# Moving filler matmuls from three carries into the last inverse of a woven recurrence, and loading o from the middle of the last gate

## The chip, the cores and the metric

The kernel runs on one core of a Trainium2 chip. The metric is the device time of one execution in microseconds (us); the time of a kernel is the median of several runs. The profiled execution is one more run, with its own time.

## The reference, cut to what matters

One layer of a diffusion backbone runs over 640 tokens (512 latent tokens of a grid, 128 context tokens) with 1024 features. A projection of the normalised input feeds two branches: an RWKV-7 recurrence in two directions over 8 heads, and a neighbourhood attention over 8 heads. Two gates scale the branches before they are added; a feed-forward network follows.

```python
u_rw, u_na, gate_rw, gate_na = split(h @ w_in)
o_rw, s_new = rwkv_branch(u_rw, ...)          # forward and backward scan, group norm, bonus, gate
o_na = na_latent(...) / na_context(...)
merged = sigmoid(gate_rw) * (o_rw @ w_o_rwkv) + sigmoid(gate_na) * (o_na @ w_o_na)
x = x + g1 * (merged @ w_out)
x = x + g2 * ((silu(h2 @ w1) * (h2 @ w3)) @ w2)
```

All products are held to float32 accuracy: every operand is split into a high and a low part of a reduced type, and a product is three matmuls (high by high, high by low, low by high).

## The kernel before, in words

**Stages.** The first stage normalises the input and makes `h`, held as a high tile `hh` and a low tile `hl` of 128 x 8 x 640 (eight blocks of 128 features, kt 0 to 7). The second does the attention. The third is the recurrence, from about 258 to 676 us of the span, and the change lies there. Then come the output projection and the feed-forward network, to the end.

**The recurrence** works in four passes (`ct` 0 to 3), one per pair of heads. The scan is done in blocks of 64 tokens, in four parts for each pass, written out in program order:

- `main`: products of keys with keys (L1126).
- `inv`, the *inverse*: 30 steps on VectorE that invert the triangular blocks (L1250 and L1254: a multiply and an add for every step), beside them three *jobs* of small matmuls on TensorE (L1145 to L1199, results masked by VectorE in L1157 and L1160), and at its end transposes (L1263, L1265) and two rounds of small matmuls, L1276 and L1290, with copies by ScalarE and VectorE between them.
- `carry`: eight steps that hand the state from block to block. In a step TensorE multiplies (L1324), ScalarE copies (L1327), TensorE multiplies (L1351), ScalarE copies (L1357), TensorE multiplies (L1364), VectorE scales the state (L1376), and the next step begins. Beside it goes `prep`, the preparation of the next pass, on ScalarE and VectorE with some matmuls; `last` finishes it at the last step.
- `out`: the normalised output of the pass (L1396, L1065, L1079, L1410). It is woven into the next pass's inverse; that of the last pass follows the last carry. It stores its chunk to DRAM (`o_d`), for passes 0 to 2; the chunk of the last pass, `o3`, stays in SBUF.

**The filler.** TensorE would stand idle for much of these chains, so a stream of other work (`stream`, `fill`) is woven in. Its units stand in `order`: projections `k`, `r`, `v` of each pass, which must be done before that pass needs them; sixteen gates `g0` to `g15` of 48 matmuls, which read `h`; eight merges `a` of 24 matmuls and eight merges `b` of 18, which read `o`, the outputs of the two branches. A unit has a weight load (`wdma`, from SyncE's queue), a cast to a high and a low part (`wcast`; by `wl` the low part comes from a subtraction on VectorE, `d`, or from an adding DMA on GpSimd's queue, `p`), its matmuls (L197), and an evaluation on ScalarE (gates, L543, stored to `tna_d` or `trw_d` by L544) or VectorE (merges, L1464 and L1467, with the gate loaded back into one of two buffers `mx`, L1450). Casts are issued one unit ahead, loads two units ahead.

**How it is woven.** `weave` walks through the yields of a part; for each it takes one entry of `plan`, whose first number says how many filler matmuls to issue there, and whose others say how far to go on with `out`, `bonus` or `prep`. For a carry the entries go in threes, one for each yield of a step. TensorE, VectorE, ScalarE and GpSimd execute in this program order; the order of SyncE's queue is chosen by the framework's scheduler. When the passes are done, `need` issues what is left of the stream without anything between.

**Where `o` lies.** `o` is a pair of tiles, high and low, in the same memory as `hh` and `hl`: `hilo` gives the same two buffers of 8 blocks. Blocks 0 to 3 are the attention's output, 4 to 6 the first three passes' output. `o_load(0, 6)` is issued when the last gate's matmuls are done (the unit before `a0`), and its DMAs wait until TensorE has read `hh` and `hl` for the last time; `o_load(6, 7)` follows when the third pass's output is stored.

**After the stream,** `last_gen` multiplies the last chunk (L1576, on `o3`) and evaluates it with VectorE (L1577, L1579), woven with the output projection.

Of the kernel before, what the change touches and what calls it, by code (L numbers as in the profile page):

```python
# [7 lines left out]
F32 = mybir.dt.float32  # L8
F32R = mybir.dt.float32r
AF = mybir.ActivationFunctionType  # L10
# [4 lines left out]
P = 128  # L15
NT = 640
NS = 512
H2 = 320
# [6 lines left out]
TCARGS = dict(schedule_with_timeline_sim=True)  # L25

PRM = dict(
    order=("l0 l1 k0 r0 v0 l2 g0 g1 g2 k1 g3 r1 g4 g5 v1 g6 g7 k2 r2 g8 g9 v2 g10 g11 k3 r3 g12 g13 v3 g15 g14 a0 a1 a2 a3 a4 a5 a6 a7 "
     "b0 b1 b2 b4 b3 b5 b6 b7"),
    plan=(  # L30
        "22.0 0.0 2.0 4.0",
        ("0.0.0 2.0.0 2.0.1 10.0.0 2.0.0 2.0.1 2.0.1 2.0.1 2.0.1 2.0.1 10.0.0 2.0.0 2.0.0 10.0.0 2.0.0 2.0.0 "
         "2.0.0 10.0.0 2.0.0 2.0.0 2.0.0 2.0.0 2.0.0 2.0.0 2.0.0 2.0.0 2.0.0 2.0.0 2.0.0 2.0.0 5.0.0 24.0.0 "
         "20.0.0 10.0.0 8.0.0 8.0.0 0.0.0"),
        ("10.0 1.0 12.1 0.2 0.0 8.1 6.2 0.0 8.1 6.2 0.0 8.1 12.2 0.0 8.1 6.2 0.0 8.1 6.2 0.0 7.1 5.2 0.0 9.1 "
         "6.2 6.0"),
        "22.0 2.0 2.0 2.0",
        ("0.0.0 0.0.0 2.0.1 10.0.0 1.0.0 2.1.1 2.1.1 2.1.1 2.1.1 1.1.1 10.0.0 3.0.0 2.0.0 2.0.0 2.1.0 2.1.0 "
         "2.0.0 10.0.0 2.0.0 2.1.0 2.1.0 2.1.0 2.1.0 2.1.0 12.1.0 2.1.0 2.1.0 2.1.0 2.0.0 2.1.0 5.0.0 24.0.0 "
         "20.0.0 10.0.0 8.0.0 8.0.0 0.0.0"),  # L40
        ("10.0 0.0 8.1 6.2 0.0 8.1 6.2 0.0 8.1 6.2 0.0 8.1 6.2 0.0 8.1 6.2 0.0 7.1 6.2 0.0 8.1 6.2 0.0 8.1 "
         "6.2 6.0"),
        "22.0 2.0 0.0 5.0",
        ("0.0.0 10.0.0 2.0.1 10.0.0 2.0.0 2.1.1 2.1.1 2.1.2 2.1.1 2.1.0 10.0.0 2.0.0 2.0.0 2.0.0 2.1.0 2.1.0 "
         "2.0.0 10.0.0 2.0.0 2.1.0 2.1.0 3.1.0 4.1.0 2.1.0 2.1.0 2.1.0 2.1.0 4.1.0 2.1.0 2.0.0 5.0.0 24.0.0 "
         "18.0.0 8.0.0 9.0.0 8.0.0 0.0.0"),
        ("10.0 0.0 8.1 14.2 0.0 8.1 6.2 0.0 8.1 6.2 0.0 0.1 6.2 0.0 8.1 6.2 0.0 8.1 6.2 0.0 8.1 6.2 0.0 8.1 "
         "6.2 6.0"),
        "22.2 0.0 4.0 6.0",
        ("0.0.0 16.1.0 8.1.1 9.0.0 2.1.0 8.1.1 8.1.1 8.1.1 8.1.1 0.1.1 0.1.0 0.0.0 0.1.0 0.1.0 0.1.0 0.1.0 "  # L50
         "6.1.0 7.1.0 6.1.0 6.0.0 6.0.0 6.0.0 0.0.0 6.0.0 6.0.0 7.0.0 6.0.0 6.0.0 6.0.0 6.0.0 6.0.0 6.0.0 "
         "11.0.0 8.0.0 8.0.0 2.0.0 0.0.0"),
        ("10.0 0.0 8.1 6.2 0.0 8.1 4.2 0.0 8.1 6.2 0.0 8.1 6.2 0.0 8.1 6.2 0.0 8.1 6.2 0.0 8.1 6.2 0.0 8.1 "
         "14.2 6.0"),
        "2 0 6 6 6 4 4 5 2 0 5 1 1 0 0"),
    qp=((0, 0, 7, 6, 7), (2, 5, 4, 4, 3, 2, 5, 3, 1)), ada=2, pa=1, pd=0,
    lw=(0, 0, 0, 0, 0, 2, 2, 2, 2, 2, 2, 2, 2, 2, 2, 2),
# [50 lines left out]
def body(ctx: ExitStack, tc: tile.TileContext, xs, xp, cols, consts, w_ada, b_row, w_rw, w_qkv,  # L108
# [3 lines left out]
    pe, act, dve, pool, sp = nc.tensor, nc.scalar, nc.vector, nc.gpsimd, nc.sync  # L112
# [12 lines left out]
    hp = right_pool(hstack, "hp")  # L125
# [9 lines left out]
    def nm(s):  # L135
        cn[0] += 1
        return f"{s}_{cn[0]}"
# [72 lines left out]
    halves = ((0, H2), (H2, NT))  # L210
# [11 lines left out]
    tna_d = dp.tile([8, P, NT], F32, name="tna_d")  # L222
# [89 lines left out]
    weights(ctx, WST, 2)  # L312
    o, mt = [], []

    def hilo(n):
# [219 lines left out]
    def gate_gen(i, w, ps_, gsb, gtag):  # L535
        dst = trw_d[i] if i < 8 else tna_d[i - 8]
        for (a, b) in ((0, H2), (H2, NT)):
            t = gsb.tile([P, H2 if gtag == "fl" else 643], F32, tag=gtag, bufs=2, name=nm(gtag))[:, :H2]
            ps = ps_()
            yield from feat_gen(ps, w, (hh, hl), 8, a, b)  # L540

            def rest(t=t, ps=ps, a=a, b=b):
                act.activation(t, ps[:, :H2], AF.Tanh, scale=0.5)  # L543
                sp.dma_start(dst[:, a:b], t)  # L544

            later(rest)

    def c64(ap, d=0):
# [171 lines left out]
    def unit(g, e):  # L720

        i, eng = int(g[1:]), eng_of(e)
        if g[0] in "ab":
            return 24 if g[0] == "a" else 18, lambda: merge_load(g[0], i), \
                lambda wt: merge_cast(*wt, eng), lambda w: merge_gen(g[0], i, w)
        if g[0] == "g":
            return 48, lambda: wdma(w_rw[15 + i]), lambda w: wcast(w, eng), \
                lambda w: gate_gen(i, w, flps, sb, gtag[-1])
# [305 lines left out]
    with ExitStack() as s3:  # L1034
# [395 lines left out]
        def o_load(a, b):  # L1430

            if not o:
                o.extend(hilo("o"))
            for q in range(a, b):
                for t, t_d in zip(o, o_d):
                    sp.dma_start(t.bitcast(F32)[:, q, :], t_d[q])

        def mt_tile(c8):
            if c8 < 4:
# [268 lines left out]
    u = {}  # L1708
# [290 lines left out]
```

## Time and profile before

| | us |
|---|---|
| median of 3 runs | 1192.29 |
| lowest, highest | 1192.16, 1193.37 |
| profiled execution | 1191.72 |
| its span | 1189.7 |
| TensorE busy in it | 1124.1 |
| VectorE busy | 777.5 |
| ScalarE busy | 530.5 |
| mean granted TensorE clock | 0.985 |

A row of the page's groups, of the order in time or of the waits names the line of the kernel, the engine (PE is TensorE, PEld its weight loads, DVE VectorE, ACT ScalarE, POOL GpSimd, SP SyncE), the operation, and output <- inputs; in the order in time the first two numbers are start and length, in us from the span's start, and brackets hold the idle time of the engine before the row and what ended it. Rows that follow each other are merged, `xN` counts them. A row of a window gives its length, the busy time of PE, PEld, DVE, ACT and POOL (with instruction counts), the granted TensorE clock, the share of time that the DMA engines were busy, and GB/s.

### The profile page before, as it was taken

Reading aid. Unit: us, or ns where it says so; the run is one execution under the profiler, and the core shown is the slowest. Engines: PE = TensorE matmul, PEld = TensorE weight load, DVE = VectorE, ACT = ScalarE, POOL = GpSimd, SP = SyncE. Lnnn points to the kernel's source line nnn. Section 1 sums busy time; section 2 is a strip of 40 time slices with the busy share of each in tenths; the row PEclk is TensorE's granted clock in tenths of the full one; section 3 lists DMA queues with packets and bytes.
Section 4 is the critical chain, followed back from the end, with each engine's and each line's share of the span. In section 5 each row is a group of like instructions: output and inputs, shape, how many; then the busy total and the mean of one; then the engine's idle time right before and its main releaser. Section 6 shows DMA issues by size and latency. Waiting matters only on the chain.

```text
span 1189.7 us, 26921 instructions
## 1 busy us (share of the span) xinstructions
PE 1124.1 (94%) x11160; PEld 998.3 (84%) x11160; DVE 777.5 (65%) x1630; ACT 530.5 (45%) x1053; POOL 205.1 (17%) x273
## 2 busy tenths in 40 slices
PE   6999999999999999999599799989999999999998
PEld 4688877789888988888488678889899989998997
DVE  4564455559469658836474675888568757775675
ACT  4444666554564664565133342654224422442340
POOL 1162244320111211111101250100001000000000
PEclk9999999999999999999799999999999999999999
DMA  9762767553333514433654851312312231232122
GB/s 335 265 117 84 244 216 230 191 146 98 103 93 84 153 50 104 123 93 79 200 138 110 245 218 54 107 49 79 104 57 86 89 107 54 89 100 90 59 75 103
DMA packets 61906, 149.42 MB, mean 126 GB/s; under 512 B 7732, under 2 KB 23732, under 8 KB 61784
## 3 DMA queue, kind: packets, MB, share of 16 engines
q1 hardware_dynamic: 55592, 131.56, 33.6%
q0 software_dynamic: 5328, 14.94, 6.8%
q8 instruction: 88, 1.44, 0.5%
q10 hardware_dynamic: 864, 1.20, 0.3%
q14 instruction: 34, 0.28, 0.1%
HBM read 118.41 MB, written 14.32 MB: 112 GB/s over the span
## 4 chain that ended last, share of the span: by engine, by line
PE 65%; DVE 8%; ACT 3%; DMA 2%; issue 1%; SPq 0%; ACTq 0%; DVEq 0%; POOLq 0%
PE f L1718 23%; PE acc L284 17%; PE fl L197 13%; DMA wlo<-wst 1%; DVE pr L1250 1%; PE w L1324 1%; PE w L1351 1%; DVE RL L1254 1%; PE mm L197 1%; PE w L1364 1%; PE w L1336 1%; PE w L1148 1%; DMA o<-o_d 1%; PE w L1196 1%; PE w L1126 1%
## 5 line engine op out<-in xcount | busy, mean ns | idle before, releaser
L1718 PE MATMUL f<-t,whi 128*128 128x320 f32 x640 | 141.4, 309 | 0.0
L1718 PE MATMUL f<-b,whi 128*128 128x320 f32 x608 | 136.5, 312 | 3.6 <-ACT b L185 1.8
L284 PE MATMUL acc<-whi,u 128*128 128x512 f32 (+1 forms) x448 | 136.0, 385 | 0.0
L197 PE MATMUL fl<-h,whi 128*128 128x320 f32 x704 | 126.5, 319 | 0.8 <-issue 0.8
L197 PEld LDWEIGHTS fl<-h,whi 128*128 128x128 f32 x704 | 106.1, 188 | 5.6 <-issue 0.9
L173 ACT CAST whi<-wst 128x1024 fp32r<-128x1024 f32 (+2 forms) x86 | 81.5, 953 | 64.7 <-PE acc L284 32.5
L1718 PEld LDWEIGHTS f<-t,whi 128*128 128x128 f32 x640 | 107.1, 188 | 0.0
L1718 PEld LDWEIGHTS f<-b,whi 128*128 128x128 f32 x608 | 103.0, 190 | 4.8 <-ACT b L185 2.2
L1718 PE MATMUL f<-t,wlo 128*128 128x320 f32 x320 | 98.9, 309 | 0.0
L284 PEld LDWEIGHTS acc<-whi,u 128*128 128x128 f32 x448 | 83.5, 188 | 16.7
L1718 PE MATMUL f<-b,wlo 128*128 128x320 f32 x304 | 94.7, 312 | 1.4 <-DVE wlo L1762 1.4
L1759 ACT CAST whi<-ws 128x1024 fp32r<-128x1024 f32 x40 | 42.0, 1051 | 108.7 <-PE f L1718 48.5
L1773 POOL TENSOR_TENSOR ws<-wst 128x512 f32<-128x512 f32 x20 | 28.2, 1409 | 341.3 <-DVE wlo L1762 226.7
L175 DVE TENSOR_TENSOR wlo<-wst,whi 128x1024 fp32r<-128x1024 f32 (+1 forms) x49 | 62.0, 1274 | 37.2 <-ACT whi L173 36.6
L284 PE MATMUL acc<-wlo,u 128*128 128x512 f32 (+1 forms) x224 | 86.3, 385 | 0.0
L284 PE MATMUL acc<-whi,h 128*128 128x512 f32 x240 | 78.0, 399 | 1.2 <-DVE h L398 1.1
L172 POOL DMA_DIRECT2D wlo<-wst x37 | 32.6, 881 | 232.4 <-ACT wlo L171 212.9
L1558 DVE SCALAR_TENSOR_TENSOR tt<-acc,G 128x512 f32<-128x512 f32 (+1 forms) x51 | 34.7, 681 | 50.5 <-PE acc L284 50.5
L197 PE MATMUL fl<-h,wlo 128*128 128x320 f32 x352 | 66.5, 321 | 0.0
L197 PE MATMUL fl<-o,whi 128*128 128x320 f32 x224 | 46.3, 337 | 16.8 <-DMA o<-o_d 10.0
L1759 ACT CAST whi<-wst 128x1024 fp32r<-128x1024 f32 (+1 forms) x48 | 41.3, 869 | 42.3 <-PE acc L284 37.6
L1718 PEld LDWEIGHTS f<-t,wlo 128*128 128x128 f32 x320 | 60.1, 188 | 0.0
(333 smaller groups left out, 2539.1 us busy)
## 6 DMA issues: line engine op xcount, KB each, us to landing
wst<-in_w_dram SPq DMA_DIRECT2D x66, 512.0 KB
wst<-in_w_rw_dram SPq DMA_DIRECT2D x31, 512.0 KB
wa<-in_w_ada_dram SPq DMA_DIRECT2D x24, 512.0 KB
wlo<-wst POOLq DMA_DIRECT2D x22, 512.0 KB, 4.5
f<-in_w_ada_dram SPq DMA_DIRECT2D x16, 512.0 KB
wst<-in_w_qkv_dram SPq DMA_DIRECT2D x12, 512.0 KB
o<-o_d SPq DMA_DIRECT2D x14, 320.0 KB
x<-in_xs_dram SPq DMA_DIRECT2D x8, 512.0 KB
```

The lines of the kernel that those rows point to most:

```text
L172: pool.dma_start(lo[:, :n].bitcast(F32), st[:, :n], accum_op=ALU.add)
L173: act.copy(hi[:, :n], st[:, :n])
L175: dve.tensor_tensor(out=lo[:, :n], in0=st[:, :n], in1=hi[:, :n].bitcast(F32), op=ALU.subtract)
L197: pe.matmul(ps[:, :t1 - t0], w[:, a:a + 128], x[:, k0 + kt, t0:t1], start=n == 0, stop=n == 3 * nk - 1)
L284: pe.matmul(pss[i][:, a:b], lhs(x, kt, ts_), w[:, cs_], start=ki == 0 and n == 0, stop=ki == last and n == 2)
L1126: pe.matmul(t[r0:r0 + 32, 64 * i:64 * i + 64], S.BK[l // 10][own, l % 10, 0, 32 * bk:32 * bk + 32], V(AG[own, l, h, :], [[0, 2], [1, 32]], ...
L1148: pe.matmul(pr[h][hrows[h ^ i], o_], x[hrows[h], :], R_[hrows[h], l, :], start=True, stop=True)
L1196: pe.matmul(pt[h][hrows[h ^ i], o_], S.BK[l // 10][hrows[h], l % 10, i, :], idh(h), start=True, stop=True)
L1558: dve.scalar_tensor_tensor(out=tt, in0=ps[:, a:b], scalar=c, in1=G[:, g, sl], op0=ALU.mult, op1=ALU.mult)
L1718: pe.matmul(ps[:, :H2], w_[:, c_], x_[:, kt, :], start=first and kt + n == 0, stop=last and kt == 3 and n == 2, skip_group_check=more)
L1759: act.copy(r[0][:, :width], src())
L1773: eng_x(PRM["se"][i - 1]).tensor_tensor(out=o_, in0=x, in1=y, op=op)
```

## The change

Four edits go together.

The plan's entries for the first three carries are two fillers lower at nearly every place (108 matmuls in all); the entries of the last pass's `main` and inverse are written anew: four at nearly every step of the inverse, 44 behind the last step. `order` brings `v1`, `k2`, `v2`, `k3`, `v3` forward among the gates, so that each projection still comes in time.

`hilo` no longer gives one tile of eight blocks but two of four (`hp_t`), behind a small class `Two` that indexes them as one.

The last gate, `g14` (`lg=14`), is issued by `gate2_gen`: it goes by blocks, both halves of the tokens for kt 0 and 1, then for 2 and 3, and so on, with three matmuls for every block, instead of one half of the tokens after the other. After its first 24 matmuls it calls `o_load(0, 4)`; `o_load(4, 6)` is called at its end.

`wl` has the low parts of the weights of all eight `b` merges made by VectorE instead of the adding DMA, and that of `a4` the other way round.

```diff
-     order=("l0 l1 k0 r0 v0 l2 g0 g1 g2 k1 g3 r1 g4 g5 v1 g6 g7 k2 r2 g8 g9 v2 g10 g11 k3 r3 g12 g13 v3 g15 g14 a0 ...
+     order=("l0 l1 k0 r0 v0 l2 g0 g1 g2 k1 g3 r1 g4 v1 g5 g6 k2 r2 g7 v2 g8 g9 k3 r3 g10 v3 g11 g12 g13 g15 g14 a0 ...
...
-        ("10.0 1.0 12.1 0.2 0.0 8.1 6.2 0.0 8.1 6.2 0.0 8.1 12.2 0.0 8.1 6.2 0.0 8.1 6.2 0.0 7.1 5.2 0.0 9.1 "
-         "6.2 6.0"),
+        ("6.0 1.0 8.1 0.2 0.0 6.1 4.2 0.0 6.1 4.2 0.0 6.1 10.2 0.0 6.1 4.2 0.0 6.1 4.2 0.0 5.1 5.2 0.0 "
+         "7.1 4.2 4.0"),
...
-        "22.2 0.0 4.0 6.0",
-        ("0.0.0 16.1.0 8.1.1 9.0.0 2.1.0 8.1.1 8.1.1 8.1.1 8.1.1 0.1.1 0.1.0 0.0.0 0.1.0 0.1.0 0.1.0 0.1.0 "
-         "6.1.0 7.1.0 6.1.0 6.0.0 6.0.0 6.0.0 0.0.0 6.0.0 6.0.0 7.0.0 6.0.0 6.0.0 6.0.0 6.0.0 6.0.0 6.0.0 "
-         "11.0.0 8.0.0 8.0.0 2.0.0 0.0.0"),
+        "22.3 0.1 4.1 6.2",
+        ("0.0.0 4.1.0 4.1.1 4.1.1 4.1.1 4.1.1 4.1.1 4.1.1 4.1.1 4.1.0 4.1.0 4.1.0 4.0.0 4.0.0 4.0.0 "
+         "4.0.0 4.0.0 4.0.0 4.0.0 4.0.0 4.0.0 4.0.0 4.0.0 4.0.0 4.0.0 4.0.0 4.0.0 4.0.0 4.0.0 4.0.0 "
+         "4.0.0 44.0.0 0.0.0 6.0.0 6.0.0 12.0.0 0.0.0"),
...
-    wl="dddddddddppppppppppppppppppppppppppdpppppppppppp", nu=9, jo=(2, 0, 1), na=(
+    wl="dddddddddppppppppppppppppppppppppppppppdddddddd", nu=9, lg=14, jo=(2, 0, 1), na=(
...
+    def hp_t(n, i, j):
+        return hp.tile([P, 4, NT], F32R, tag=f"hp{i}{j}", bufs=1, name=f"{n}{i}{j}")
...
     def hilo(n):
-        return [hp.tile([P, 8, NT], F32R, tag=f"hp{i}", bufs=1, name=f"{n}{i}") for i in range(2)]
+        return [Two([hp_t(n, i, j) for j in range(2)]) for i in range(2)]
...
+    def gate2_gen(i, w, ps_, gsb, gtag):
+        dst = trw_d[i] if i < 8 else tna_d[i - 8]
+        ps = [ps_(), None]
+        for kts in ((0, 1), (2, 3), (4, 5), (6, 7)):
+            for hf, (a, b) in enumerate(halves):
+                if ps[hf] is None:
+                    ps[hf] = ps_()
+                for kt in kts:
+                    for n, (u, x) in enumerate(((w[0], hh), (w[0], hl), (w[1], hh))):
+                        pe.matmul(ps[hf][:, :H2], u[:, kt * 128:kt * 128 + 128], x[:, kt, a:b],
+                                  start=kt == 0 and n == 0, stop=kt == 7 and n == 2)
+                        yield
+            if kts[1] == 3:
+                o_load(0, 4)
...
                     if i + 1 < len(order) and order[i + 1] == "a0":
-                        o_load(0, 6)
+                        o_load(4, 6)
...
         def o_load(a, b):
             if not o:
-                o.extend(hilo("o"))
+                o.extend(Two([]) for _ in range(2))
             for q in range(a, b):
-                for t, t_d in zip(o, o_d):
-                    sp.dma_start(t.bitcast(F32)[:, q, :], t_d[q])
+                for i, (t, t_d) in enumerate(zip(o, o_d)):
+                    if len(t.ts) == q // 4:
+                        t.ts.append(hp_t("o", i, q // 4))
+                    sp.dma_start(t[:, q, :].bitcast(F32), t_d[q])
```

The other two carries' entries change in the same way as the one shown.

More of the change, by code (lines that the diff above doesn't have):

```diff
@@ L27 @@
 PRM = dict(
[L28 to L29 removed]
+    order=("l0 l1 k0 r0 v0 l2 g0 g1 g2 k1 g3 r1 g4 v1 g5 g6 k2 r2 g7 v2 g8 g9 k3 r3 g10 v3 g11 g12 g13 g15 g14 a0 a1 a2 "
+     "a3 a4 a5 a6 a7 b0 b1 b2 b4 b3 b5 b6 b7"),
     plan=(
         "22.0 0.0 2.0 4.0",
[L32 to L54 removed]
@@ new lines @@
+        ("8.0 0.0 6.1 4.2 0.0 6.1 4.2 0.0 6.1 4.2 0.0 6.1 4.2 0.0 6.1 4.2 0.0 5.1 4.2 0.0 6.1 4.2 0.0 "
+         "6.1 4.2 4.0"),
+        "22.0 2.0 0.0 5.0",
+        ("0.0.0 10.0.0 2.0.1 10.0.0 2.0.0 2.1.1 2.1.1 2.1.2 2.1.1 2.1.0 10.0.0 2.0.0 2.0.0 2.0.0 2.1.0 "
+         "2.1.0 2.0.0 10.0.0 2.0.0 2.1.0 2.1.0 3.1.0 4.1.0 2.1.0 2.1.0 2.1.0 2.1.0 4.1.0 2.1.0 2.0.0 "
+         "5.0.0 24.0.0 18.0.0 8.0.0 9.0.0 8.0.0 0.0.0"),
+        ("6.0 0.0 6.1 12.2 0.0 6.1 4.2 0.0 6.1 4.2 0.0 0.1 4.2 0.0 6.1 4.2 0.0 6.1 4.2 0.0 6.1 4.2 0.0 "
+         "6.1 4.2 4.0"),
@@ L313, in body, with __init__, __getitem__ @@
     o, mt = [], []
+    def hp_t(n, i, j):
+        return hp.tile([P, 4, NT], F32R, tag=f"hp{i}{j}", bufs=1, name=f"{n}{i}{j}")
+    class Two:
+        def __init__(self, ts):
+            self.ts = ts
+        def __getitem__(self, x):
+            return self.ts[x[1] // 4][x[0], x[1] % 4, x[2]]
     def hilo(n):
-        return [hp.tile([P, 8, NT], F32R, tag=f"hp{i}", bufs=1, name=f"{n}{i}") for i in range(2)]
+        return [Two([hp_t(n, i, j) for j in range(2)]) for i in range(2)]
     hh, hl = hilo("h")
@@ L546, in gate_gen, with rest @@
             later(rest)
+    def gate2_gen(i, w, ps_, gsb, gtag):
[12 more added lines that the diff above has]
+                o_load(0, 4)
+        def rest(hf, a, b):
+            t = gsb.tile([P, H2 if gtag == "fl" else 643], F32, tag=gtag, bufs=2, name=nm(gtag))[:, :H2]
+            act.activation(t, ps[hf][:, :H2], AF.Tanh, scale=0.5)
+            sp.dma_start(dst[:, a:b], t)
+        for hf, (a, b) in enumerate(halves):
+            later(lambda hf=hf, a=a, b=b: rest(hf, a, b))
     def c64(ap, d=0):
```

10 lines of the change are left out of this document (9 added, 1 removed).

## The prediction

> **What bounds the kernel now.** I read the page first, then PE's waits, then PE's order in time through the recurrence, and last the sums of a few stretches. Every time below is us.
>
> The page: busy shares, and the span in 40 slices of 29.7.
>
> ```profile
> PE 1124.1 (94%) x11160; PEld 998.3 (84%) x11160; DVE 777.5 (65%) x1630; ACT 530.5 (45%) x1053; POOL 205.1 (17%) x273
> PE   6999999999999999999599799989999999999998
> PEclk9999999999999999999799999999999999999999
> ```
>
> TensorE is the bound almost everywhere. After the start, the slices that are not full are those from 565 to 595, 654 to 684 and their neighbours: the last inverse, and the end of the recurrence. In the first of them the clock was low too. PE's waits name what was late (line, releaser, total, times, longest):
>
> ```profile
> PE fl L197 <- DMA o<-o_d: 10.0, 1, 10.0
> PE fl L197 <- DVE mt L1464: 4.7, 1, 4.7
> PE fl L1576 <- ACT o L185: 3.1, 1, 3.1
> PE w L1324 <- DVE ZV L1376: 1.5, 1, 1.5
> PE w L1351 <- ACT x L1327: 1.4, 4, 0.4
> PE w L1364 <- ACT ZV L1357: 0.4, 1, 0.4
> ```
>
> The first two lie in the last inverse, the third at the recurrence's end; the last three are all that the carries wait. Four stretches summed (length, busy PE, weight loads, DVE, ACT, POOL, then the granted clock): the third pass's inverse, the fourth's, a busy carry step, and the stretch from the fourth carry's end to the first matmul on the last chunk of `o`.
>
> ```profile
> 449.38:500.51 51.13, 47.87 (x1013) 44.10 (x1012) 44.28 (x151) 27.93 (x54) 8.61 (x18) 1.00 0.38 103
> 550.22:621.94 71.72, 54.91 (x1032) 50.38 (x1031) 46.46 (x158) 22.84 (x47) 11.22 (x15) 0.88 0.53 155
> 427.72:432.65 4.93, 4.49 (x63) 3.77 (x62) 1.13 (x3) 4.30 (x12) 1.03 (x2) 1.00 0.63 140
> 661.48:679.03 17.55, 12.67 (x81) 11.30 (x80) 9.98 (x20) 6.62 (x14) 5.29 (x4) 1.00 0.86 251
> ```
>
> The fourth inverse does what the third does, with 24 filler matmuls more (208 against 184, counted in the order of issue), and takes 20.6 longer: it waits, and part of it runs at half clock. That is the loss that the change can reach.
>
> **The unit of the sum.** What moves is filler: 128x128 by 320 matmuls. Twelve of them back to back, from the first row's start to the second's:
>
> ```profile
> 599.16 1.33 PE L197 MATMUL fl<-o,whi 128*128 128x320 f32 x8
> 600.92 1.33 PE L197 MATMUL fl<-o,whi 128*128 128x320 f32 x8
> ```
>
> 1.76 for 12 is 0.147 each. The order of issue of both kernels gives the counts. The first three inverses and carries lose 5+32, 2+34 and 4+44 fillers, 121 in all (108 is what the plan takes out; the rest is a knock-on of the stream's own order). The last inverse keeps 208, but 175 of them are gates (54 before) and 33 merges (154 before). The last carry keeps 126. What follows it has 177 merges instead of 56. No matmul is added or dropped, so the change moves 121 x 0.147 = 17.8 of PE work from the first three carries to the end of the recurrence, and the time changes only by waits.
>
> **First three carries: -17.8 + 5.** A carry step is a ring: L1324 on PE, a copy on ACT, L1351, two copies on ACT (L1357), L1364, two multiplies on DVE (L1376), the next L1324. Filler covers the second and third hand-over: 8 and 6 before, 6 and 4 after. In a quiet step of the fourth carry:
>
> ```profile
> 636.94 0.45 PE L1324 MATMUL w<-ZV,AG 128*64 128x64 f32 x8
> 638.31 0.55 ACT L1357 COPY ZV<-w 64x128 f32<-64x128 f32 x2 [0.55 <-PE w L1351]
> 639.55 0.45 PE L1364 MATMUL w<-ZV,TG 128*64 128x64 f32 x8
> 640.05 0.61 DVE L1376 TENSOR_TENSOR ZV<-w,Dt 64x128 f32<-64x128 f32 x2 [2.81 <-PE w L1364]
> 641.25 0.45 PE L1324 MATMUL w<-ZV,AG 128*64 128x64 f32 x8
> ```
>
> ACT is done at 638.86 and PE takes the result at 639.55: 0.69 in hand. DVE is done at 640.66, PE goes on at 641.25: 0.59. Two fillers less take 0.29 from each, so a quiet step shortens from 4.31 to 3.7 without a wait. The first three carries are not quiet: the next pass's preparation queues on ACT and DVE. In the busy step above ACT works 4.30 of 4.93 and PE already waits 0.44 of it; with four fillers less PE needs 3.9, and the step will not go below ACT's 4. Nearly all steps elsewhere have room, so I charge 0.2 on each of 24 steps, 5 in all. The bounds: nothing (the quiet step), and all 17.8 (a rival below).
>
> **Last inverse: -14.7.** Gates read `h`, which is there; merges read `o`, which must come from DRAM into the place of `h`. Before, the load could start only as the last gate ended:
>
> ```profile
> 562.20 8.15 SPq L1436 DMA_DIRECT2D o<-o_d  x12
> 573.93 3.07 PE L197 MATMUL fl<-o,whi 128*128 128x320 f32 x7 [10.04 <-DMA o<-o_d]
> 574.72 0.50 PEld L197 LDWEIGHTS fl<-o,whi 128*128 128x128 f32 x2 [0.29 <-DMA o<-o_d]
> 576.36 0.29 PEld L197 LDWEIGHTS fl<-o,whi 128*128 128x128 f32 x1 [0.30 <-DMA o<-o_d]
> ```
>
> The six loads of the low halves went out ahead of the first high half, so PE had its first pair only at 573.9; from then a load landed every 0.81 (574.72 to 576.36 are two). Everything in PE's order behind the first merge waited with it, the output step of the third pass (L1079) and so DVE with its inverse among it. After, gates fill this inverse nearly to its end. The two new tiles of four blocks are free after 24 matmuls of the last gate, and eight loads go out in pairs. Between that point and the first merge PE has 24 gate matmuls (3.5) and the small ones of L1276 (1.5, first row below), so 5.0. The first load lands no sooner than a small transfer does (second row, the last number), and no later than the rows above allow:
>
> ```profile
> 612.20 1.47 PE L1276 MATMUL w<-f,Nt 32*32 32x32 f32 x80
> wlo<-wst POOLq DMA_DIRECT2D x8, 192.0 KB, 3.9
> ```
>
> 3.9 from issue to landing, or 11.7 for seven loads less six at 0.81, 6.8. The eighth is then there 9.6 to 12.5 after the release. Without waits PE would want it at about 6, so it waits 3.6 to 6.5; I take 4, near the lower end because these loads find the queue empty. ACT would hold PE nearly as long at this place: the next matmuls (L1290) need four copies of L1276's results, and among them ACT's order has two gate outputs and the next merge's two casts: eight operations of about the size of this one, some 4 together:
>
> ```profile
> 638.88 0.53 ACT L171 ACTIVATE wlo<-wst 128x384 fp32r<-128x384 f32 x1
> ```
>
> The two waits run side by side and are counted once.
>
> The inverse then costs the third one's PE work, 47.9, 24 fillers more (3.5), the wait (4), and 1.6 for what follows a wait, below: 57.0 against 71.7. DVE does not forbid that: 44.28 busy in the third inverse, which holds projections of the next pass that the fourth has not. Bounds: 53 (hardly a wait) and 61 (6.5, half clock and some of the third inverse's own 3.3 of waits).
>
> SP's queue holds the fourteen loads in one run, ahead of the last gate's stores and the weights of the third merge. The first two merges, 48 fillers woven into the inverse's end and the carry's start, cover those weights, and POOL adds their low parts as before. I cost this at nothing; without that cover PE would wait for one such addition, up to 3.9 less what is left of the merges.
>
> **What a wait costs beside itself.** Two stretches of one window each, with busy PE and clock:
>
> ```profile
> 341.80:345.20 3.40, 1.87 (x25) 1.43 (x23) 2.56 (x6) 3.33 (x6) 0.86 (x1) 1.00 0.02 5
> 345.20:348.60 3.40, 3.40 (x30) 3.03 (x30) 2.38 (x4) 2.23 (x6) 0.00 (x0) 0.51 0.78 154
> 614.90:618.30 3.40, 2.06 (x39) 1.86 (x43) 3.35 (x8) 0.51 (x2) 0.00 (x0) 1.00 0.39 100
> ```
>
> A wait of 1.53 was followed by 3.4 at half clock; 1.34 idle left the clock whole. So 3.4 at half clock, 1.7 of work lost, follows a wait of about 1.5 in such a window; 0.2 a step does not bring it, the wait for `o` may, hence the 1.6. The Trainium skill, "TensorE: Matmul & The Clock Gate", section "What's actually happening", has the array fall to half rate only after at least one idle window of about 3.4. The trace differs, since 1.53 idle was enough here; by the Trainium skill's rule the sum would be 1.6 lower, and I go by the rows.
>
> **End of the recurrence: +17.8 - 3.3 + 2 = +16.5.** The 121 merges come as one block with nothing woven in. Before, PE waited for the last chunk of `o` at the end, and DVE was behind with weights:
>
> ```profile
> 675.34 0.60 PE L197 MATMUL fl<-o,wlo 128*128 128x320 f32 x3
> 680.41 1.21 DVE L175 TENSOR_TENSOR wlo<-wst,whi 128x1024 fp32r<-128x1024 f32 x1
> 681.55 1.27 DVE L1577 SCALAR_TENSOR_TENSOR pre<-pre,fl 128x320 f32<-128x320 f32 x3
> ```
>
> From the last merge's end (675.94) to DVE's first step of the next stage (681.55) passed 5.6. After, the chunk is long ready when the block ends; DVE has one weight split (1.21) and two steps of 0.49 left, 2.3 with the first matmuls. That returns 3.3. The block itself is 7.7 units of 18 matmuls (2.65). A unit's DVE work is four steps and a split, which moves from a POOL addition to DVE:
>
> ```profile
> 663.05 0.49 DVE L1464 SCALAR_TENSOR_TENSOR mx<-mx,fl 128x320 f32<-128x320 f32 x1 [1.38 <-PE fl L197]
> 663.57 0.49 DVE L1467 TENSOR_TENSOR mt<-mt,mx 128x320 f32<-128x320 f32 x1
> 601.94 0.68 DVE L175 TENSOR_TENSOR wlo<-wst,whi 128x512 fp32r<-128x512 f32 x1
> ```
>
> 4 x 0.49 + at most 0.68 is 2.6, as long as PE's: level, so 0.25 a unit, 2 in all (0 to 10, second rival).
>
> **Sum.** -17.8 + 5 - 14.7 + 16.5 = -11.0. The profiled execution took 1191.7, its span 1189.7; the median of the runs is 1192.3. -11.0 gives 1181.3 on the median. The inverse's bounds give 4 to either side, half of the carries' lower bound and of an equal step above 2.5, the block 1 (its 10 is a rival): 1174 to 1189 for the forecast alone.
>
> **Rivals.**
> 1. The split load buys little: `o` still lands 10 late, as in the old row. Then the inverse is 47.9 + 3.5 + 10 + 1.7, 63.1, and the time 1187.4. For it: the same 2.6 MB at the same rate. Against: five of the ten are covered by PE work behind the release, and the pairs are ordered.
> 2. The closing block is paced by transfers. Two `mx` buffers make a ring over two units: load, then DVE's 2.6. At 3.9 a load it is 3.3 a unit, at 5, 3.8; with 5 the block loses 1.15 x 7.7 = 8.9 instead of 2: 1188.2. For it: the stretch from 661 had DMA at 0.86. Against: the loads for the next stage come before the block now.
> 3. The carries keep their length, and it gets slower. If ACT's queue paces the steps, removed filler becomes waiting, all 17.8 of it: 12.8 more than forecast, 1194.1, and the two later carries, which end without a wait today, each bring a window at half clock as the first does: 1197.5. It decides where the steps lose over 0.66 each on average. For it: the busy step. Against: the quiet one has 0.59 and 0.69 in hand, and over a whole carry ACT has room:
>
> ```profile
> 405.00:448.00 43.00, 42.32 (x572) 37.29 (x569) 21.26 (x38) 28.20 (x72) 7.39 (x11) 1.00 0.32 81
> ```
>
> 28.2 of 43, which 36 fillers less (5.3) leave at 28.2 of 38 at the most.
>
> **Chances.** Forecast 0.68, rivals 0.10, 0.10 and 0.12. From no change a measurement here can tell about 0.2%, 2.4. Faster: the forecast and the first two rivals without their tails, 0.86; slower: most of the third, 0.10; the same, 0.04. The range for 8 in 10 takes the forecast's own, the first two rivals, and 2 below it for terms that fall together: 1172 to 1190.
>
> **What would show it.** Right: the wait for `o` at 3 to 6 in pieces, late in an inverse of about 57; carry steps of 3.7 to 4.4 with small waits on L1327, L1357, L1376; a block of 138 merges of about 22 behind the last output step; no wait on the last chunk. Wrong: half clock inside the first three carries, an `o` wait near 10, or PE waiting for DVE or `mx` through the block.

## The result, and the profile after

| | before | after |
|---|---|---|
| median of 4 runs, us | 1192.43 | 1200.47 |
| lowest, highest | 1192.16, 1193.37 | 1199.02, 1202.57 |
| profiled execution, its span | 1191.72, 1189.7 | 1199.02, 1197.2 |

The changed kernel is slower: ratio 1.0066, 95% interval 1.0051 to 1.0081, some 8 us. The forecast was 1181.3 in 1172 to 1190.

The page of the changed kernel, its busy times and the same two rows of slices (29.9 us each):

```profile
PE 1130.5 (94%) x11160; PEld 1003.5 (84%) x11160; DVE 778.9 (65%) x1637; ACT 527.9 (44%) x1046; POOL 196.3 (16%) x266
PE   6999999999998998899989989999999999999998
PEclk9999999999999998899989999999999999999999
```

The hole in the last inverse (565 to 595 before) has closed, and so has the one at the recurrence's end but for a digit. But where the page before has nines, eights have come: from 359 to 389 and, in the clock too, from 449 to 509. Those lie in the second and the third inverse. (The eights from 599 to 629 belong to the end of the last inverse; the one from 688 to 718 lies in the last chunk and what follows it.) (The passes are counted from one here: the inverses of passes one to four are the first, second, third and last inverse.)

The recurrence in stretches (length, busy PE, weight loads, DVE, ACT, POOL, clock, DMA share, GB/s). Of before, the first carry, second inverse, second carry and third carry, which the prediction did not show:

```profile
305.23:354.86 49.63, 47.49 (x625) 41.93 (x624) 23.63 (x44) 29.75 (x75) 6.14 (x10) 0.97 0.33 86
354.86:403.09 48.23, 46.56 (x1009) 43.22 (x1008) 43.94 (x150) 27.02 (x53) 10.13 (x21) 1.00 0.42 109
403.09:449.38 46.29, 45.53 (x619) 40.11 (x618) 24.21 (x43) 28.57 (x73) 7.83 (x12) 1.00 0.35 90
500.51:550.22 49.71, 48.57 (x636) 42.77 (x635) 23.61 (x44) 29.54 (x76) 7.16 (x12) 1.00 0.36 93
```

Of after, from the first carry to the last inverse without a gap, and then the stretch from the last carry's end to the first matmul on the last chunk of `o`:

```profile
304.94:351.54 46.60, 43.22 (x592) 37.50 (x591) 23.47 (x45) 28.03 (x72) 6.78 (x12) 0.96 0.25 66
351.54:405.06 53.52, 48.49 (x1006) 44.77 (x1005) 46.58 (x153) 26.57 (x53) 7.48 (x17) 0.97 0.38 102
405.06:448.02 42.96, 40.64 (x585) 35.07 (x584) 21.26 (x39) 27.63 (x71) 8.18 (x12) 1.00 0.25 68
448.02:509.75 61.73, 51.94 (x1008) 48.09 (x1008) 47.34 (x154) 26.29 (x52) 8.82 (x20) 0.89 0.37 95
509.75:554.63 44.88, 43.17 (x602) 37.46 (x602) 23.61 (x43) 29.87 (x76) 5.99 (x11) 1.00 0.32 80
554.63:613.12 58.49, 53.24 (x1022) 48.18 (x1021) 40.63 (x144) 22.54 (x44) 8.21 (x13) 0.91 0.56 170
651.68:686.06 34.38, 31.80 (x202) 30.59 (x201) 23.51 (x49) 9.41 (x18) 3.94 (x3) 0.95 0.66 202
```

Set against each other, in us:

| stretch | before | after | change | forecast |
|---|---|---|---|---|
| three carries | 145.6 | 134.4 | -11.2 | -12.8, inverses' 11 fillers included |
| second and third inverse | 99.4 | 115.3 | **+15.9** | in the line above |
| last inverse | 71.7 | 58.5 | -13.2 | -14.7 |
| last carry's end to the last chunk | 17.6 | 34.4 | +16.8 | +16.5, with what follows it |
| all the rest | | | -0.8 | 0 |

The rest is the span's difference, 7.5, less the lines above. Three lines came near the forecast. The miss stands in two inverses that the sum took as unchanged but for a few fillers. By the rows above, 9.9 of their 15.9 is TensorE idle (14.8 for 4.9) and 6.0 is longer busy time: some 17 of the two inverses ran at half clock (clock 0.97 and 0.89), and none of them before. TensorE's waits (line, releaser, total, times, longest) name what is late in them:

```profile
PE w L1182 <- DVE out L1446: 8.3, 3, 3.6
PE fl L197 <- issue: 4.5, 2, 3.5
PE fl L1612 <- DVE tr L1613: 3.3, 1, 3.3
PE w L1385 <- ACT x L1361: 3.2, 5, 1.0
PE fl L197 <- DMA o<-o_d: 2.2, 5, 0.6
PE w L1358 <- DVE ZV L1410: 2.1, 2, 1.8
PE fl L197 <- DMA wlo<-wst: 1.8, 1, 1.8
```

Lines of the kernel's part on the recurrence are 34 higher than before: L1182 is L1148, the third job's matmuls; L1446 is L1412, the last multiply of the output step; L1160 is L1126, the tiny matmuls of `main`. The wait between these two was 2.0 in all before, a row that the list of waits in the prediction leaves out:

```profile
PE w L1148 <- DVE out L1412: 2.0, 1, 2.0
```

The 10.0 on `o` has become 2.2. The 4.5 on "issue", a wait for nothing that the profile shows, has a piece of 3.5.

**The first of the two.** VectorE in the third inverse (start, length):

```profile
485.00 0.34 DVE L533 SCALAR_TENSOR_TENSOR kt__622<-U,C,kt__622 128x128 f32<-128x128 f32 x1
...
485.71 0.74 DVE L533 SCALAR_TENSOR_TENSOR kt__622<-U,C,kt__622 128x512 f32<-128x512 f32 x1
486.49 0.75 DVE L535 SCALAR_TENSOR_TENSOR kt__622<-U,C,kt__622 128x512 f32<-128x512 f32 x1
487.16 0.48 DVE L1446 TENSOR_TENSOR out<-w,out 128x320 f32<-128x320 f32 x1
...
490.21 0.48 DVE L1446 TENSOR_TENSOR out<-w,out 128x320 f32<-128x320 f32 x1
```

and TensorE there:

```profile
487.70 0.33 PE L1182 MATMUL w<-R__2889,f 64*64 64x64 f32 x2 [2.02 <-DVE out L1446]
490.74 0.38 PE L1182 MATMUL w<-R__2889,f 64*64 64x64 f32 x3 [2.71 <-DVE out L1446]
```

L533 and L535 are the four steps that shift the projection `k3` by a token, 2.2 together. They stand ahead of both L1446; L1446 empties a PSUM buffer `w`; the third job's matmuls wait for one. (In the second inverse the steps of `k2`, at 383.3 to 385.5, stand ahead of the second L1446 alone, and its wait of 3.6 follows.) Before, the same steps came behind both L1412, here in the third inverse:

```profile
482.37 0.48 DVE L1412 TENSOR_TENSOR out<-w,out 128x320 f32<-128x320 f32 x1
...
486.88 0.35 DVE L522 SCALAR_TENSOR_TENSOR kt__620<-U,C,kt__620 128x128 f32<-128x128 f32 x1 [0.31 <-ACT kt__620 L521]
```

In fillers: `k2` ended at the 85th of its inverse before and at the 74th after, `k3` at the 102nd and at the 79th. `order` moved `k2` one gate of 48 fillers forward and `k3` two, while the passes ahead of them had lost only 37 and 73 fillers.

**The second.** The order in time of all engines, three rows:

```profile
447.33 0.88 POOL L172 DMA_DIRECT2D wlo<-wst  x1 [1.73 <-ACT wlo L171]
...
451.48 0.46 PE L1160 MATMUL w<-AG,f 64*32 64x64 f32 x32
...
455.45 1.49 PE L197 MATMUL fl<-h,wlo 128*128 128x320 f32 x5 [3.51 <-issue]
```

The matmul at 455.45 needs nothing new. What the trace does have is TensorE's program being loaded: DMA queue q8 moves 88 blocks of 16 KiB in the execution, one for every 256 of TensorE's 22,517 records (weight loads, matmuls and some 200 semaphore instructions). The queues (packets, MB, share) from 443.5 to 452.9, with the adding DMA's time to landing, and from there to 454.1:

```profile
q0 software_dynamic: 144, 0.52, 35.4%
q1 hardware_dynamic: 280, 0.48, 13.6%
q14 instruction: 1, 0.01, 0.5%
...
wlo<-wst POOLq DMA_DIRECT2D x1, 512.0 KB, 5.6
```

```profile
q1 hardware_dynamic: 19, 0.05, 29.4%
q8 instruction: 1, 0.02, 5.0%
```

No block for TensorE arrives in the first stretch. The adding DMA (q0) landed at 452.9; the block was loaded from 453.02 to 453.97, and 1.48 later TensorE went on. It had stopped behind record 10177, 193 past a multiple of 256.

### The profile page after: what moved, and what is told of

The parts are those of the page before. It is cut to its first block, busy times and chain, and to the rows that moved or that the text cites. A ratio compares the mean times of both kernels' runs of the same rounds, so it can differ in the third digit from the quotient of the medians.

```text
span 1197.2 us, 26923 instructions
## 1 busy us (share of the span) xinstructions
PE 1130.5 (94%) x11160; PEld 1003.5 (84%) x11160; DVE 778.9 (65%) x1637; ACT 527.9 (44%) x1046; POOL 196.3 (16%) x266
## 4 chain that ended last, share of the span: by engine, by line
PE 51%; DVE 4%; DMA 2%; ACT 2%; issue 2%; SPq 1%; POOL 0%; DVEq 0%; ACTq 0%; POOLq 0%
PE f L1754 21%; PE acc L284 16%; PE fl L197 8%; DMA wlo<-wst 1%; DMA tr<-trw_d 1%; DMA o<-o_d 1%; PE w L1182 1%; DVE hq L1713 0%; PE w L1398 0%; PE w L1358 0%; DVE t L186 0%; PE w L1385 0%; PE w L1370 0%; PE w L1230 0%; PE w L1415 0%
## 5 line engine op out<-in xcount | busy, mean ns | idle before, releaser
L197 PE MATMUL fl<-h,whi 128*128 128x320 f32 x672 | 122.1, 323 | 1.0 <-issue 1.0
L197 PEld LDWEIGHTS fl<-h,whi 128*128 128x128 f32 x672 | 103.2, 191 | 5.4 <-issue 1.2
L175 DVE TENSOR_TENSOR wlo<-wst,whi 128x1024 fp32r<-128x1024 f32 (+1 forms) x56 | 65.1, 1169 | 36.6 <-ACT whi L173 36.1
L1594 DVE SCALAR_TENSOR_TENSOR tt<-acc,G 128x512 f32<-128x512 f32 (+1 forms) x51 | 34.7, 680 | 51.1 <-PE acc L284 51.1
L172 POOL DMA_DIRECT2D wlo<-wst x30 | 26.5, 882 | 238.8 <-ACT wlo L171 234.8
L1754 PEld LDWEIGHTS f<-b,wlo 128*128 128x128 f32 x304 | 57.4, 189 | 2.5 <-DVE wlo L1798 2.5
```

Of the source, the lines that this page charges most:

```text
L172: pool.dma_start(lo[:, :n].bitcast(F32), st[:, :n], accum_op=ALU.add)
L175: dve.tensor_tensor(out=lo[:, :n], in0=st[:, :n], in1=hi[:, :n].bitcast(F32), op=ALU.subtract)
L197: pe.matmul(ps[:, :t1 - t0], w[:, a:a + 128], x[:, k0 + kt, t0:t1], start=n == 0, stop=n == 3 * nk - 1)
L1594: dve.scalar_tensor_tensor(out=tt, in0=ps[:, a:b], scalar=c, in1=G[:, g, sl], op0=ALU.mult, op1=ALU.mult)
L1754: pe.matmul(ps[:, :H2], w_[:, c_], x_[:, kt, :], start=first and kt + n == 0, stop=last and kt == 3 and n == 2, skip_group_check=more)
```

## The experiments

All ratios are to the kernel before on the same chip, with 95% intervals. The two inverses are given as second / third, against 48.2 / 51.1 before and 53.5 / 61.7 after. They are read from one profiled execution each, and half clock moves them: the third inverse of e7 and e8, whose program there is the changed kernel's, took 59.3 and 59.5, with 6.8 at half clock instead of 13.7. A difference of 2 in a third inverse says little. The runs e1 to e3 and e5 to e10 start from the changed kernel. Where two runs are set against each other, it is by their medians; the kernel before had medians of 1192.3 to 1193.4 beside them, so 1 of such a difference can be the chip's.

**e1: later shifts.**

```diff
+        lag = 24 if ci in (6, 7) else 0
-        later(lambda: shift(512, 640, 514), (0.4, 0.7), 2)
-        later(lambda: shift(0, 512, 1), (0.8, 1.5), 5)
+        later(lambda: shift(512, 640, 514), (0.4, 0.7), 2 + lag)
+        later(lambda: shift(0, 512, 1), (0.8, 1.5), 5 + lag)
```

> The changed kernel, with the four shift steps on VectorE of k2 and k3 issued 24 fillers-or-steps later, so that in the second and third inverses they stand behind the output step's last multiply (L1446) again, as they do before the change. Theory (the new order put 2.2 us of VectorE work ahead of L1446, and TensorE's third job waits for the PSUM buffers that L1446 frees): the wait of L1182 for L1446 falls from 8.3 in three to about 2 in one, the second inverse from 53.5 to 48-50, the third from 61.7 to 56-58, the time from 1200.5 to 1191-1194. Rival (the inverses are longer because TensorE now reaches them earlier and meets VectorE's chain, wherever the shifts stand): the wait moves to another VectorE step, and the time stays within 2 of 1200.5.

1200.2, ratio 1.0044 (1.0028 to 1.0059); 56.0 / 55.4. The wait for L1446 fell to 2.8 (about 2 was expected), but waits for weights rose from 1.8 to 6.9: `later` is a queue, and the casts of the next weights stood behind the shifts. Neither theory is decided.

**e2: matmuls put in front of TensorE's program,** so that its blocks end elsewhere.

```diff
+    for _ in range(120):
+        pe.matmul(psa[:16, :16], mhalf[:32, :16], mhalf[:32, :16], start=True, stop=True)
```

> The changed kernel, with 120 matmuls of 32x16 by 16 (240 instructions, no use made of their result) ahead of TensorE's first, while it waits for its first weights. They move every later instruction by 240 places against the 256-instruction blocks in which TensorE's program is loaded. Theory (the 3.5 us wait in the third inverse that the profile puts down to issue is TensorE out of instructions: the load of a block of 16 KiB started only at 453.0, behind an adding DMA): the wait goes or moves elsewhere, the third inverse is 4 to 5.5 shorter with its half clock (3.5 and half of 3.4), and the time falls by 3 to 6, less up to 1 if the added matmuls reach past TensorE's first wait. Rival (the wait belongs to the data or to VectorE): it stays at its place with its length, and the time is that of the changed kernel or up to 1 more.

1202.7, ratio 1.0072 (1.0046 to 1.0098); 52.7 / 55.6. The trace has the 120 calls as 240 weight loads and 240 matmuls: the program moved by 480 places, not by the 240 of the expectation, and the first product of the kernel's own starts at 9.3 instead of 6.8. The wait in the third inverse is gone, and that inverse is 6.2 shorter. The time did not fall, since one of 2.2 came in the last inverse and a longer one in the first, in the middle of a run of L1162 (L1160 of after):

```profile
265.39 1.76 PE L1162 MATMUL w<-AG,f 64*32 64x64 f32 x156
272.98 0.32 PE L1162 MATMUL w<-AG,f 64*32 64x64 f32 x2 [5.82 <-issue]
```

Another adding DMA was under way there, from 264.0 to 270.0, and the block was loaded from 270.55 to 271.57. So the wait belongs to the place in the program, not to the data: the theory holds, its gain does not.

**e3: both.** The two edits together.

> The changed kernel with the later shifts of k2 and k3 and with the 240 instructions in front. If both theories hold, the second and third inverses are within 2 of what they were before the change (48.2 and 51.1), and the time is 1185-1189, faster than the kernel before: the carries' 11 and the last inverse's 13 stand against the 17 of the end. If only the first holds, 1191-1194; if only the second, 1195-1197; if neither, 1200.

1206.5, ratio 1.0104 (1.0082 to 1.0126); 53.8 / 57.3. A miss: 5.8 in the first inverse on the block, as in e2, and 7.7 on weights, as in e1.

**e4: the part on `o` alone, in the kernel before.** `hp_t`, `Two`, `gate2_gen` and the new `o_load`, nothing else; against before:

```diff
...
-                        o_load(0, 6)
+                        o_load(4, 6)
...
-                lambda w: gate_gen(i, w, flps, sb, gtag[-1])
+                lambda w: (gate2_gen if i == PRM["lg"] else gate_gen)(i, w, flps, sb, gtag[-1])
```

> The kernel before, with only the part on o of the change: tiles of four blocks, the last gate by blocks, the first four blocks of o loaded from its middle on; plan, order and weights as before. Theory (the wait of 10.0 for o in the last inverse is shortened by what TensorE does between the release and the first merge, about 5): the wait is 4 to 6, the last inverse 63-67 instead of 71.7, the time 1185-1189. Rival (the load is bound by its own length, wherever it starts, since merges follow at once and want the sixth block 1.8 after the first): waits of about 10 in pieces, 1190-1193.

1187.9, ratio 0.9947 (0.9927 to 0.9967): faster. The wait for `o` is 2.5 in five pieces, below the 4 to 6, but the inverse, 68.1, is still long: a wait of 4.7 for merges and 13.7 at half clock remain.

**e5: later shifts in a list of their own,** so that nothing queues behind them.

```diff
...
+        if ci in (6, 7):
+            late.append([off[0] + 26, lambda: shift(512, 640, 514)])
+            late.append([off[0] + 29, lambda: shift(0, 512, 1)])
+            return
```

> The changed kernel with the shifts of k2 and k3 behind the output step's last multiply, as in the run with later shifts, but kept in a list of their own, so that the casts of the next weights no longer queue behind them. Theory (those later shifts did take the wait for L1446 away, and gave it back as 6.9 of waiting for weights whose casts stood behind them): the waits are about 2.8 for L1446 and at most 2 for weights, the second inverse 48-50, the third 55-57 (the wait put down to issue stays, 2.9 to 3.5, and what it brings in half clock), the time 1193-1195.5. Rival (the inverses have no room, whatever is late): 1199-1201.

1196.1, ratio 1.0025 (1.0005 to 1.0045); 54.2 / 57.4. 4.4 better than the changed kernel, less than expected. The waits are 2.8 for L1446 (L1455 here) and 3.7, not 2, for weights:

```profile
PE w L1191 <- DVE out L1455: 2.8, 2, 1.4
PE fl L197 <- DMA wlo<-wst: 3.7, 3, 1.9
```

GpSimd's order in time shows why:

```profile
391.01 0.10 POOL L522 MEMSET U<- 128x2 f32 x1 [7.09 <-DVE kt__622 L540]
...
391.58 0.88 POOL L172 DMA_DIRECT2D wlo<-wst  x1 [0.43 <-PE fl L197]
```

The late shift holds the buffer `U`, GpSimd waits 7.1 to clear it for the next projection, and the adding DMA of the weights is behind that in its order.

**e6: e5, and the cast of `k3`'s weights later.**

```diff
-                if j == n // 8:
+                if j == (24 if order[i + 1:i + 2] == ["k3"] else n // 8):
```

> The same, and the cast of k3's weights called at the 25th filler of the gate before it instead of at the 7th, so that its adding DMA (512 KB, 447.3 to 452.9 in the changed kernel) starts behind the tiny matmuls of L1160 instead of ahead of them. Theory (TensorE runs out of instructions there, since the load of its next block waits for that DMA): the wait put down to issue in the third inverse goes, that inverse is 50.5-53, the time 3 to 5 below the run beside it, 1188.5-1191.5. Rival (the block's load is late for another reason, or the wait is not for instructions): the wait stays at the same place, and the time is that of the run beside it.

1194.8, ratio 1.0010 (0.9989 to 1.0031); 53.3 / 53.6. The third inverse is 3.8 shorter and the wait on its block 1.7 instead of 3.4, not gone. Two medians 1.3 apart, each within 2.5 to either side, don't prove a gain in time. Nor do the 3.8, since 6.8 at half clock in e5's third inverse did not come here.

**e7: the changed kernel without its part on `o`.** `lg=99` gives the last gate back to `gate_gen`.

```diff
-        return [Two([hp_t(n, i, j) for j in range(2)]) for i in range(2)]
+        return [hp.tile([P, 8, NT], F32R, tag=f"hp{i}", bufs=1, name=f"{n}{i}") for i in range(2)]
...
-                        o_load(4, 6)
+                        o_load(0, 6)
```

> The changed kernel without its part on o: tiles of eight blocks, the last gate one half of the tokens after the other, all of o loaded behind it; plan, order and weights as changed. Theory (the last inverse owes its 13 less to gates in place of merges and to the early load together): the first merge waits 8 to 10 for o, the last inverse is 64-68 instead of 58.5, the time 1206-1210. Rival (the gates alone do it, since the merges now come at the inverse's end): the wait is under 4, the time within 2 of 1200.5.

1201.9, ratio 1.0066 (1.0042 to 1.0090): the time is the rival's, not to be told from the changed kernel's, and below the 1206 to 1210 of the theory. The theory's wait is there,

```profile
PE fl L197 <- DMA o<-o_d: 8.7, 2, 7.5
```

but the last inverse is 61.8, only 3.4 longer than with the early load. In this plan most of the last inverse's gain comes from gates in the place of merges.

**e8: `wl` as before the change.**

```diff
-    wl="dddddddddppppppppppppppppppppppppppppppdddddddd", ...
+    wl="dddddddddppppppppppppppppppppppppppdpppppppppppp", ...
```

> The changed kernel with the weights' low parts made as before the change (those of the b merges by the adding DMA, that of a4 by VectorE). Theory (the closing block of merges is paced by TensorE or VectorE, 2.65 a unit): VectorE saves 0.68 a unit and nothing waits, the stretch from the last output step to the last chunk stays at 33-35, the time within 1.5 of 1200.5. Rival (an adding DMA of some 4 for a unit of 2.65 paces the block): 7 units lose 1.2 each, the stretch is 40-43, the time 1207-1209.

1207.5, ratio 1.0104 (1.0055 to 1.0154): the rival. The stretch of the closing block:

```profile
652.01:696.34 44.33, 35.98 (x203) 33.76 (x201) 18.96 (x40) 12.44 (x25) 10.90 (x11) 0.88 0.74 190
```

44.3 instead of 34.4, with five waits for weights, 8.1 in all, and 10.2 at half clock: here a block of merges with nothing between is paced by the adding DMAs, and the edit of `wl` is needed for it. (The two times' intervals overlap; the claim rests on the waits and the stretch.)

**e9: the shifts of `k2` and `k3` left out on VectorE.**

```diff
+            if ci in (6, 7):
+                return
             dve.scalar_tensor_tensor(out=o, in0=U[:, u - 1:u - 1 + n], ...
```

> The changed kernel with the eight multiply-add steps on VectorE that shift k2 and k3 left out (so k2 and k3 are not the reference's); nothing is put off, no buffer is held longer. Theory (those steps, standing ahead of L1446, are what lengthens the second inverse, and 4 to 5 of the third): the wait for L1446 is at most 2.8, the second inverse 48-50, the third 55-57 with the wait put down to issue still in it, the time 1190-1193; the runs with put-off shifts stayed above that because the shifts then held the buffer that GpSimd clears ahead of the next adding DMA. Rival (the inverses have no room after shorter carries): 1195 or more.

1192.2, ratio 0.9991 (0.9972 to 1.0009): 8.2 below the changed kernel, as expected. The waits for L1446 (L1448 here) are 3.5, not 2.8 at most:

```profile
PE w L1184 <- DVE out L1448: 3.5, 2, 2.1
```

The inverses are 50.3 / 58.0, a little above what was expected (the profiled execution was this kernel's slowest, with 10.2 at half clock in the third inverse).

**e10: e9, without the adding DMA for `k3`.**

```diff
-            pool.dma_start(lo[:, :n].bitcast(F32), st[:, :n], accum_op=ALU.add)
+            if not skip:
+                pool.dma_start(lo[:, :n].bitcast(F32), st[:, :n], accum_op=ALU.add)
...
-        return 48, lambda: wdma(w_rw[ci]), lambda w: wcast(w, eng), \
+        return 48, lambda: wdma(w_rw[ci]), lambda w: wcast(w, eng, g == "k3"), \
```

> The same, and the adding DMA for k3's weights left out (their low part is then wrong). Theory (that DMA holds back the load of TensorE's next block of instructions): the wait put down to issue in the third inverse, 3.5, goes with the half clock behind it, the third inverse is 50-53, the time 4 to 6 below the run beside it, 1185-1188, so the two together make up what the prediction missed. Rival: the wait stays, the time within 1 of the run beside it.

1187.1, ratio 0.9942 (0.9927 to 0.9957): 5.1 below e9. The inverses:

```profile
350.79:400.56 49.77, 46.91 (x1006) 43.30 (x1005) 43.90 (x149) 26.36 (x53) 7.48 (x17) 1.00 0.41 107
444.95:499.46 54.51, 48.48 (x1008) 44.95 (x1007) 44.73 (x150) 26.01 (x52) 8.18 (x17) 0.97 0.35 99
```

The time is as expected; the third inverse is longer than the 50 to 53, since the wait on the block shrank only to 2.4. The load still started 2.2 after TensorE entered the block before. Other transfers were under way then (the gate of a merge and the next weights, issued at 445.2 and 445.6); that they held it back was not tested.

**e11: the third carry's matmuls alone moved.** Plan of passes one to three as before but for the third carry; last pass, `wl` and the part on `o` as changed; `order` with `v3` one gate earlier than before. Against before:

```diff
-    order="... k3 r3 g12 g13 v3 g15 g14 a0 ..."
+    order="... k3 r3 g12 v3 g13 g15 g14 a0 ..."
...
-        ("10.0 0.0 8.1 14.2 0.0 8.1 6.2 0.0 8.1 6.2 0.0 0.1 6.2 ...
+        ("6.0 0.0 6.1 12.2 0.0 6.1 4.2 0.0 6.1 4.2 0.0 0.1 4.2 ...
```

> The kernel before with the part on o and the weights as changed, the changed plan of the third carry and of the last pass only (44 matmuls moved instead of 121), and the order of before with v3 one gate earlier, so that k2 and k3 come where they came before. Theory (what was forecast holds where the inverses are left alone): the second and third inverses are 48 and 51, the third carry 45, the last inverse 58-62, the end 23-25 instead of 17.5, the time 1179-1183, the fastest so far. Rival (with 110 merges still in it, the last inverse is paced by VectorE, which evaluates them between its steps): it takes 65 or more, the time 1186-1189.

1186.1, ratio 0.9932 (0.9917 to 0.9947), the lowest median of all, though not to be told from e4's and e10's. The second and third inverse, the last one, and the closing stretch:

```profile
354.13:402.37 48.24, 46.70 (x1009) 43.35 (x1008) 43.98 (x150) 27.01 (x53) 10.12 (x21) 1.00 0.41 108
448.64:499.31 50.67, 47.26 (x1009) 43.51 (x1008) 43.69 (x150) 27.52 (x54) 8.48 (x17) 1.00 0.37 102
544.98:612.70 67.72, 56.83 (x1023) 50.57 (x1022) 43.18 (x150) 23.05 (x45) 10.14 (x15) 0.87 0.53 159
651.60:673.26 21.66, 20.08 (x129) 18.32 (x128) 17.15 (x36) 7.12 (x14) 3.93 (x3) 1.00 0.67 215
```

The inverses that are left alone are what they were. The last one gained 4.0 where 10 to 14 were expected. The rival's length came, but not for its reason: VectorE is busy 43.2 of 67.7. TensorE waits 5.3 for `o` in four pieces and 1.8 for a block of its program, and 17.1 run at half clock.

**e12: e11 with `o` in tiles of two blocks,** each freed and loaded as the last gate is done with it.

```diff
-            if kts[1] == 3:
-                o_load(0, 4)
+            if kts[1] < 6:
+                o_load(kts[0], kts[1] + 1)
```

> The run with the third carry's matmuls alone moved (1186.1), with o in tiles of two blocks instead of four: the last gate gives the first pair of blocks free after 12 of its matmuls, the second after 24, the third after 36, and o is loaded in that order. Theory (its last inverse of 67.7 still waits 5.3 for o in four pieces, and half clock follows): the first load starts 1.8 us earlier, the waits for o fall to 2-4, none over 1.3, less of the inverse runs at half clock, it takes 62-66, and the time is 1181-1185. Rival (the landing of one block after the other sets it, not the start): the waits stay near 5, the time within 1.5 of 1186.

1187.4, ratio 0.9965 (0.9950 to 0.9981): the rival. The waits for `o` are 6.2 in seven pieces, the longest 1.9, the last inverse is 66.1, and the time is no better than e11's.

## Why the prediction was wrong

**The step that failed** is the first term of the sum, "First three carries: -17.8 + 5", and the sentence ahead of it, that "the time changes only by waits". The waits were looked for in the carries and at the places where merges were moved from and to. The inverses between them were taken at their old length less their 11 fillers (1.6), and the edit of `order` was given no price at all; the second and third became 15.9 longer. It moved more than matmuls: a projection brings four VectorE steps and copies on ScalarE with it. Their place before and after was to be read from the instruction order, and the 2.0 that L1148 waited for L1412 before, in the third inverse, said that there was no room there. What it cost: without those steps the time is 8.2 lower (e9). That the place makes the wait is seen in the waits: 8.3 for L1446 with the steps ahead of it, 2.8 with the steps behind it (e1, e5), 3.5 without them (e9). How much of the 8.2 the place is worth alone stays open: e9 also leaves out 4.4 of VectorE's work, and e5, which keeps the work and gains 4.4, has 3.7 of waits for weights (1.8 in the changed kernel).

The second part, TensorE out of instructions, 3.5 and the half clock behind it, was not seen as a cost at all. e2 shows that it depends on the place in the program. e6 and e10 show that it shrinks, to 1.7 and 2.4, as the transfer ahead of the block's load is put off or left out; e10 is 5.1 below e9. Together e9 and e10 take 13.3 off the changed kernel, of the 19.2 by which it lay above the forecast. With them the two inverses are still 4.9 longer than before: 3.5 on L1446 and 2.4 on the block are still waited there, against 2.0 before. That last part was not taken apart further.

**Carries: right.** 110 of the 121 matmuls left the carries themselves, 16.2 at 0.147 each; the carries became 11.2 shorter. So 5.0 came back, as forecast: 3.4 as idle time (7.4 for 4.0), most of it in waits on ScalarE's copies (L1385, 3.2 for 1.4 before), in the next pass's preparation (L645, 1.5 for 0.6) and on VectorE's scaling (L1358, 2.1 for 1.5), and 1.6 because TensorE's busy time fell by 14.6 and not by 16.2. The third rival, carries that keep their length, is refuted, though its time, 1197.5, was the nearest. It ended on the right side by another mechanism.

**Last inverse: right in the sum, -13.2 for -14.7.** The wait for `o` was mis-sized upward: 2.2 in five pieces for 4, none over 0.6, with 1.1 on ScalarE ahead of them. The half clock was mis-sized downward: 10.2 where the term had one window of 3.4. The two errors go opposite ways, so that the sum came so near is in part luck. e7 shows that the early load carries 3.4 of the gain in length; its time does not show it.

**End: right, +16.8 for +16.5.** The closing block ran near its matmuls' pace, with 1.8 once for an adding DMA. PE no longer waits for the last chunk, but 3.3 for VectorE's L1613 behind it. That VectorE and not GpSimd makes the low parts is worth 9.9 there (e8, one execution of each). The second rival, a block paced by the gates' loads, did not come.

**Half clock by the rows.** The prediction's rows had 3.4 at half clock behind a wait of 1.5. In the third inverse half clock lasted 6.8 from the end of the 3.5 without a matmul on (454.6 to 461.4), and 6.8 more from 488.7 on, between the waits of 2.0 and 2.7 for L1446. The sum had none in this stage.

## What to carry to other kernels

Moving a unit of a woven stream moves all that the unit issues on every engine: list for each moved unit its steps on the other engines, and which waiting instruction each of them now stands ahead of. Where a stage already has a small wait for such an instruction, it has no room; that none shows is no proof of room, for the second inverse had no wait for L1412 before and 3.6 after. And a plan that gains in one place by filler from many others is better tried in parts: the part on `o` with a third of the moves (e11) beat the whole change by 14 us, and the part on `o` alone (e4, 1187.9) came within 2 of that, with no move at all.

## What the runs showed of the hardware

TensorE can run out of program. Its instructions come in blocks of 256, 16 KiB. A block's load started when TensorE had about one block left (in the changed kernel, with at most 297 instructions in hand); it took 0.9 to 1.8 where TensorE waited for it, and TensorE went on 1.2 to 1.6 after its end. In all runs, the waits on "issue" of a microsecond or more between 255 and 690 fell 193 or 194 past a multiple of 256, counting all of TensorE's records. Filler matmuls need 128 x 0.147, 19 us, for a block. The stretches with the tiny ones of L1160 pass one in 1.3 to 2.1, less than a load and the step behind it need. So even a load that started 0.7 after TensorE had entered the block before meant a wait of 1.8 (e11), and the wait follows the delay of the load: 1.7 for 1.6 (e6), 2.4 for 2.2 (e10), 3.5 for 3.2 (the changed kernel), 5.8 for 5.0 (e2), the last two behind an adding DMA. The Trainium skill, "Runtime: NRT & Kernel Launch", section "Instruction fetch mechanics", has the same block and calls the cost mostly hidden. That agrees with nearly all of the 88 loads here, and not with these.
